# The row of 1/rms: made by two transfers through HBM instead of four transposes and a copy

## The chip, the cores and the metric

The kernel runs on one core of a Trainium2 chip. The metric is the device time of one execution in microseconds, as a median over runs. Smaller is better. The engines are named as in the profile: PE multiplies matrices (TensorE), DVE and ACT do elementwise work (VectorE, ScalarE), POOL is GpSimd, and SP issues transfers.

## The reference

Two layers over 512 tokens of width 1024. Only the first half of a layer concerns the change:

```python
def rmsnorm(x, g):
    xf = x.astype(jnp.float32)
    y = xf * lax.rsqrt(jnp.mean(xf * xf, axis=-1, keepdims=True) + NORM_EPS)
    return (y * g.astype(jnp.float32)).astype(x.dtype)
...
    xn = rmsnorm(x, norm1_g[i])
    proj = xn @ w_in[i]
    u_pool, q, k, v, g_a, g_b = jnp.split(proj, splits, axis=-1)
    ...
    o = diff_attention(q, k, v, lam)
    o = rmsnorm(o, subln_g[i]) * (1.0 - lam_init)
    attn_out = o.transpose(0, 2, 1, 3).reshape(b, s, DIFF_V_WIDTH)
    pool_out = pool_mixer(u_pool, pool_w[i], pool_scale[i])
    merged = jax.nn.sigmoid(g_a) * pool_out + jax.nn.sigmoid(g_b) * attn_out
    x = x + merged @ w_out[i]
```

The pool mixer takes, for each of four groups of channels, the mean over a window of 2, 4, 8 or 16 tokens less the token's own value, and multiplies by a matrix. The attention takes the difference of two softmaxes. Behind it comes a gated feed-forward block with a norm of its own.

## The kernel before

**Products.** Every operand of a product is split in a high and a low part (`split`, L213: a cast on ACT, a subtraction on DVE), and a product is three matmuls: high by high, low by high, high by low (L308 to L310; called a triple here). The names end in h and l: `xh`, `xl` are the tokens, `whi`, `wlo` a piece of weights, `qh`, `ql` the queries and keys, `vh`, `vl` the values, `ah`, `al` the turned attention weights, `uh`, `ul` the windowed means. Weights come in pieces of 512 KB (`raw`, L225), which SP issues in program order, as far ahead as its seven buffers allow.

**The norm.** The weights multiply x itself, and the factor 1/rms of a token is applied to the product. `token_stats` makes it on POOL (L440) as `stats[0][:, 1, :]`, 128 partitions by 4 columns: token on the partition, block of 128 tokens in the column. Queries, keys, values and the attention's gate have tokens on the partitions and use it as a scale. The pool mixer's input and the gate of the pool mixer have tokens along the free dimension, so they need 1/rms as a row of 512 that is the same on all partitions: `rms_rows[layer]`, the second half of the tile `hg`. Its readers are L715 (`up`) and L749 (`ta`) in `merged`. `spread_rms` makes it, once in each layer.

**The attention** goes head by head (3, 2, 1, 0), and in a head by blocks of 128 tokens, t = 0 to 3. Queries and keys of a block are normed, rotated, transposed and scaled (`near`, L546), split to `qh` and `ql`, and `scores(t)` multiplies them; ACT takes the exponentials (L562, `pr`), DVE finishes the softmax, the result is transposed and split to `ah`, `al`, and `weighted(t)` multiplies it with the values (`vh,ah`, then `vl,ah`, then `vh,al`). Its square sum (L606, `mt`), the gate (L610) and a transpose follow, and L629 writes it to `mj`. Except at the start of the program, a transpose is made in two steps: DVE transposes blocks of 32 by 32 (L323), and SP moves the blocks to HBM and back (`turned`: `away<-near` L324, `near<-away` L328, four for each tile). `merged` of a head then makes the windowed means (`up` L715, sums `us` L720, `head` L723, L724, L726) and the two gates (`ta` L749, its tanh L753).

**What sets the order.** A clock counts the columns that PE has been given so far. `later(delay, task)` puts a task on a heap for the time clock + delay, and between triples the due ones are emitted. A scheduler then fixes the order of each engine when the program is built, from the order of emission and the dependencies; on the chip an engine works through its own list and waits at each row for its operands. So a task that is emitted earlier or later can change places with others on each engine.

Of the kernel before, what the change touches and what calls it, by code (L numbers as in the profile page):

```python
# [10 lines left out]
F32 = mybir.dt.float32  # L11
# [7 lines left out]
P = 128  # L19
# [3 lines left out]
NT = S // P  # L23
# [101 lines left out]
def trunk_kernel(  # L125
# [10 lines left out]
    nc = tc.nc  # L136
# [3 lines left out]
    hbm = ctx.enter_context(tc.tile_pool(name="hbm", bufs=1, space=bass.MemoryType.DRAM))  # L140
# [29 lines left out]
    rotary, rms_rows = {}, {}  # L170
# [5 lines left out]
    def head_gains(layer):  # L176

        g = sb.tile([P, 2, S], F32, name="hg", tag="hg")
        rms_rows[layer] = g[:, 1, :]
        cs, sn = rotary[layer] = [g[:, 0, i * VD:(i + 1) * VD].rearrange("p (a t r) -> p a t r", a=2, t=NT) for i in range(2)]  # L180
        row = sb.tile([P, 2, ROT], F32, name="gr", tag="m12")
        for a in range(2):
            nc.sync.dma_start(row[:, a, :], spread(rows[layer][R_QG + QK * a:R_QG + QK * a + ROT]))
        for a in range(2):
            def times(to, table, gains):
                nc.gpsimd.tensor_tensor(to, table, gains.unsqueeze(1).broadcast_to(list(table.shape)), op=ALU.mult)
            times(cs[:, a], cos_t, row[:, a, :])
            for h in range(2):
                here, there = slice(h * HALF, (h + 1) * HALF), slice((1 - h) * HALF, (2 - h) * HALF)
                times(sn[:, a, :, here], sin_t[:, :, here], row[:, a, there])  # L190
        nc.gpsimd.tensor_tensor(gain_column(layer, 0), gain_column(layer, 0), gain_column(layer, 1), op=ALU.mult)
        nc.gpsimd.memset(gain_column(layer, 0)[:ROT], 1.0)
# [68 lines left out]
    def later(delay, what):  # L261
        heapq.heappush(waiting, (clock[0] + delay, count[0], what))
        count[0] += 1
# [50 lines left out]
    def transpose(dst, src):  # L314
        nc.tensor.transpose(dst, src, ident)  # L315
        clock[0] += 2 * P
# [75 lines left out]
    def token(t):  # L392
        return slice(t * P, (t + 1) * P)
# [20 lines left out]
    stats = [None]  # L414
# [87 lines left out]

    def spread_rms(layer):

        row = tr_ps()
        for t in range(NT):
            transpose(row[:, token(t)], stats[0][:, 1, t:t + 1].broadcast_to([P, P]))
        nc.scalar.copy(rms_rows[layer], row)

    for layer in range(L):  # L510
        lam_init = 0.8 - 0.6 * math.exp(-0.3 * layer)
        if layer:
            head_gains(layer)
        later(81600, lambda layer=layer: spread_rms(layer))

        def x_tok(t):
            return [(xh[:, k, token(t)], xl[:, k, token(t)]) for k in range(KD)]
# [588 lines left out]
```

## Time and profile before

| | |
|---|---|
| median of 3 runs | 1378.48 us (1378.47 to 1379.03) |
| the profiled execution | 1377.74 us |
| its span | 1376.0 us, granted TensorE clock 1.000 |
| PE, DVE, ACT, POOL busy | 1370.0, 996.5, 775.1, 130.5 us |
| moved by DMA | 224.07 MB, mean 163 GB/s |

The span is the time from the first to the last event that the profile records; the execution is 1.7 us longer. A row of a timeline gives the start, the duration, the engine, the line in the kernel, the operation, and what it writes and reads; in brackets stands the idle time of its engine ahead of it and what ended it. PE starts a matmul before the one ahead of it has ended, so a matmul of 512 columns has a duration of 0.39 us, and the next one starts 0.23 us behind it. Layer 0 runs to about 700 us, layer 1 from there.

### The profile page before, as it was taken

What the parts mean: (1) busy time and instruction counts of PE and PEld (TensorE: products, weight loads), DVE (VectorE), ACT (ScalarE), POOL (GpSimd) and SP (SyncE); (2) the same over time, 40 slices, a digit from 0 to 9 for tenths busy, and PEclk for the clock granted to TensorE, in tenths of its full rate; (3) what the DMA queues carried; (4) which work ended last, traced back from release to release, by engine and by line L of the source; (5) the groups of instructions that cost most, each with busy time, mean ns of one, the idle gap of its engine ahead of it and who ended that gap; (6) DMA issues with size and microseconds to landing.
All of it is one profiled execution on the core that took longest, in us unless ns stands there. A gap on an engine that the chain in (4) does not pass through costs nothing.

```text
span 1376.0 us, 18657 instructions
## 1 busy us (share of the span) xinstructions
PE 1370.0 (100%) x6238; PEld 1138.1 (83%) x6238; DVE 996.5 (72%) x1787; ACT 775.1 (56%) x1577; POOL 130.5 (9%) x155
## 2 busy tenths in 40 slices
PE   9999999999999999999999999999999999999999
PEld 6888888888888888888888888888888888888887
DVE  7668667676968768678666786765878687686782
ACT  7665564554856545564367755556557665554540
POOL 3010100000101101010010001010001111000100
PEclk9999999999999999999999999999999999999999
DMA  8244454445668968686435455444536788687731
GB/s 312 84 143 121 139 150 143 145 128 151 126 189 193 231 182 222 172 202 189 148 107 163 125 169 166 137 129 137 167 111 139 197 211 221 184 212 175 208 123 62
DMA packets 141072, 224.07 MB, mean 163 GB/s; under 512 B 41392, under 2 KB 88496, under 8 KB 140976
## 3 DMA queue, kind: packets, MB, share of 16 engines
q1 hardware_dynamic: 130320, 186.93, 42.9%
q0 software_dynamic: 9216, 33.56, 14.2%
q10 hardware_dynamic: 1440, 2.39, 0.6%
q8 instruction: 49, 0.80, 0.2%
q14 instruction: 47, 0.39, 0.1%
HBM read 193.59 MB, written 29.23 MB: 162 GB/s over the span
## 4 chain that ended last, share of the span: by engine, by line
PE 98%; DVE 1%; DMA 0%; issue 0%; ACT 0%; SPq 0%; ACTq 0%; DVEq 0%
PE mm L290 17%; PE mm L289 17%; PE mm L291 17%; PE mm L308 15%; PE mm L309 15%; PE mm L310 15%; DMA raw<-in_wts 0%; PE mm L315 0%; DVE xl L476 0%; PE mm L438 0%; DVE wlo L213 0%; PE mm L488 0%; PE mm L486 0%; PE mm L487 0%; DVE sq L427 0%
## 5 line engine op out<-in xcount | busy, mean ns | idle before, releaser
L213 DVE TENSOR_TENSOR wlo<-raw,whi 128x1024 fp32r<-128x1024 f32 (+1 forms) x220 | 267.0, 1218 | 73.9 <-ACT whi L213 73.0
L213 ACT CAST whi<-raw 128x1024 fp32r<-128x1024 f32 (+1 forms) x220 | 229.3, 1052 | 143.8 <-PE mm L291 74.6
L308 PE MATMUL mm<-whi,xh 128*128 128x512 f32 x480 | 188.8, 393 | 0.0
L310 PE MATMUL mm<-whi,xl 128*128 128x512 f32 x480 | 187.2, 390 | 0.0
L309 PE MATMUL mm<-wlo,xh 128*128 128x512 f32 x480 | 187.1, 390 | 0.0
L289 PE MATMUL mm<-whi,xh 128*128 128x512 f32 x384 | 149.6, 390 | 0.0
L291 PE MATMUL mm<-whi,xl 128*128 128x512 f32 x384 | 149.4, 389 | 0.0
L290 PE MATMUL mm<-wlo,xh 128*128 128x512 f32 x384 | 149.4, 389 | 0.0
L290 PE MATMUL mm<-fl,whi 128*128 128x512 f32 (+1 forms) x356 | 137.6, 387 | 0.0
L291 PE MATMUL mm<-fh,wlo 128*128 128x512 f32 (+1 forms) x356 | 137.6, 387 | 0.0
L289 PE MATMUL mm<-fh,whi 128*128 128x512 f32 (+1 forms) x356 | 137.6, 387 | 0.0
L768 DVE TENSOR_TENSOR res<-mm,res 128x512 f32<-128x512 f32 (+1 forms) x145 | 97.8, 679 | 44.0 <-PE mm L291 41.8
L239 POOL DMA_DIRECT2D wlo<-in_wts x64 | 56.1, 876 | 536.6 <-ACT wlo L238 390.3
L353 POOL TENSOR_TENSOR r<-r,mhalf 128x4 f32<-128x4 f32 (+1 forms) x64 | 58.1, 910 | 512.9 <-DVE r L352 493.1
L310 PEld LDWEIGHTS mm<-whi,xl 128*128 128x128 f32 x480 | 90.1, 188 | 19.3
L309 PEld LDWEIGHTS mm<-wlo,xh 128*128 128x128 f32 x480 | 90.3, 188 | 17.3
L308 PEld LDWEIGHTS mm<-whi,xh 128*128 128x128 f32 x480 | 90.2, 188 | 17.3
L308 PE MATMUL mm<-xh,whi 128*128 128x512 f32 x256 | 99.8, 390 | 0.0
L309 PE MATMUL mm<-xl,whi 128*128 128x512 f32 x256 | 99.8, 390 | 0.0
L310 PE MATMUL mm<-xh,wlo 128*128 128x512 f32 x256 | 99.6, 389 | 0.0
L291 PEld LDWEIGHTS mm<-whi,xl 128*128 128x128 f32 x384 | 72.1, 188 | 15.0
L290 PEld LDWEIGHTS mm<-wlo,xh 128*128 128x128 f32 x384 | 72.1, 188 | 15.0
(220 smaller groups left out, 2764.0 us busy)
## 6 DMA issues: line engine op xcount, KB each, us to landing
raw<-in_wts SPq DMA_DIRECT2D x243, 512.0 KB, 4.1
wlo<-in_wts POOLq DMA_DIRECT2D x64, 512.0 KB, 6.4
away<-near SPq DMA_DIRECT2D x73, 256.0 KB, 2.3
near<-away SPq DMA_DIRECT2D x292, 64.0 KB, 2.8
away<-near SPq DMA_DIRECT2D x29, 128.0 KB, 2.0
near<-away SPq DMA_DIRECT2D x116, 32.0 KB, 2.2
pwr<-in_pool_w ACTq DMA_DIRECT2D x8, 256.0 KB, 2.8
out<-res SPq DMA_DIRECT2D x7, 256.0 KB, 2.0
```

Of the source, the lines that this page charges most:

```text
L213: return nc.scalar.copy(hi, src), nc.vector.tensor_sub(lo, src, hi.bitcast(F32))
L239: nc.gpsimd.dma_start(lo.rearrange("p a b -> p (a b)"), wts[piece_no], accum_op=ALU.add)
L289: nc.tensor.matmul(acc, lhsT=ah, rhs=bh, start=start, stop=False, **check)
L290: nc.tensor.matmul(acc, lhsT=ah, rhs=bl, start=False, stop=False, **check)
L291: last = nc.tensor.matmul(acc, lhsT=al, rhs=bh, start=False, stop=stop, **check)
L308: nc.tensor.matmul(acc, lhsT=ah, rhs=bh, start=i == 0, stop=False)
L309: nc.tensor.matmul(acc, lhsT=ah, rhs=bl, start=False, stop=False)
L310: last = nc.tensor.matmul(acc, lhsT=al, rhs=bh, start=False, stop=i == n - 1)
L353: nc.gpsimd.tensor_tensor(r, r, mhalf[:, :width], op=ALU.pow)
L768: return nc.vector.tensor_add(res[d][:, cs], acc, res[d][:, cs])
```

## The change

`spread_rms` no longer transposes on PE and copies on ACT. SP writes the 512 values to a row in HBM (128 partitions by 4 columns of 4 bytes, turned by the access pattern), and a second transfer on SP, which waits for the first to land, reads the row back onto all partitions. The task is put on the heap 64800 columns ahead in place of 81600, and the transposes' 1024 columns no longer advance the clock.

```diff
     def spread_rms(layer):
 
-        row = tr_ps()
-        for t in range(NT):
-            transpose(row[:, token(t)], stats[0][:, 1, t:t + 1].broadcast_to([P, P]))
-        nc.scalar.copy(rms_rows[layer], row)
+        row = hbm.tile([NT, P], F32, name="row", tag="row", bufs=2)
+        nc.sync.dma_start(row.rearrange("t p -> p t"), stats[0][:, 1, :])
+        nc.sync.dma_start(rms_rows[layer], row.rearrange("t p -> (t p)").partition_broadcast(P))
 
     for layer in range(L):
         lam_init = 0.8 - 0.6 * math.exp(-0.3 * layer)
         if layer:
             head_gains(layer)
-        later(81600, lambda layer=layer: spread_rms(layer))
+        later(64800, lambda layer=layer: spread_rms(layer))
```

The lines below are one shorter, so L606 of before is L605 of the changed kernel. The order of the engines changes with it. On SP, in layer 1, where the queries and keys of the first head are sent away, it was:

```order
L225 DMA raw<-in_wts 128x1024 x2
L328 DMA near<-away 32x4x128 x4
L225 DMA raw<-in_wts 128x1024 x9
L324 DMA away<-near 128x512 x2
L328 DMA near<-away 32x4x128 x8
```

and it is now:

```order
L225 DMA raw<-in_wts 128x1024 x2
L328 DMA near<-away 32x4x128 x4
L225 DMA raw<-in_wts 128x1024 x9
L506 DMA row<-stats 128x4x1
L507 DMA hg<-row 128x512
L324 DMA away<-near 128x512 x2
L328 DMA near<-away 32x4x128 x8
```

The two transfers stand ahead of the first two away-transfers. In layer 0 they stand among the weight pieces: four pieces and two other loads, the write, two pieces, the read, eleven pieces.

On ACT, in layer 1, second head, around the cast of `ah` for `weighted(2)` (128x384), with the tanh of the first gate `ta` and the casts of both halves of `uh`, it was:

```order
L606 ACTIVATE mt,sso<-mm 128x256
L213 CAST uh<-us 128x512
L213 CAST ah<-pr 128x384
L213 CAST uh<-us 128x512
L606 ACTIVATE mt,sso<-mm 128x256
L753 ACTIVATE ta<-ta 128x512
L213 CAST whi<-raw 128x1024 x3
L213 CAST ah<-pr 128x512
```

and it is now:

```order
L605 ACTIVATE mt,sso<-mm 128x256
L568 ACTIVATE rc<-st 128x1
L213 CAST uh<-us 128x512
L752 ACTIVATE ta<-ta 128x512
L213 CAST ah<-pr 128x384
L213 CAST uh<-us 128x512
L605 ACTIVATE mt,sso<-mm 128x256
L213 CAST whi<-raw 128x1024
L213 CAST ah<-pr 128x512
```

The tanh has moved from behind this cast to ahead of it. On PE the same place was, from the end of the product that the gate `ta` reads to the first matmuls of `weighted(2)`:

```order
L308 MATMUL mm<-xh,whi 128x512
L309 MATMUL mm<-xl,whi 128x512
L310 MATMUL mm<-xh,wlo 128x512
L308 MATMUL mm<-vh,ah 128x256
L309 MATMUL mm<-vl,ah 128x256
L308 MATMUL mm<-xh,whi 128x512
L309 MATMUL mm<-xl,whi 128x512
L310 MATMUL mm<-xh,wlo 128x512
L310 MATMUL mm<-vh,al 128x256
```

and it is now:

```order
L308 MATMUL mm<-xh,whi 128x512
L309 MATMUL mm<-xl,whi 128x512
L310 MATMUL mm<-xh,wlo 128x512
L308 MATMUL mm<-vh,ah 128x256
L309 MATMUL mm<-vl,ah 128x256
L310 MATMUL mm<-vh,al 128x256
```

The triple that stood between the matmuls of `ah` and that of `al` has gone behind them. On DVE, in the same place, the subtraction `al` stood ahead of the multiply `ta` (L749); now `ta` (L748) comes first, then the last window sum, `head` and the two rows that finish `us`, and then `al`.

On ACT, in the same head around the cast of `qh` for `scores(1)`, it was:

```order
L692 ACTIVATE vh<-mm,stats 128x256
L695 ACTIVATE tb<-mm,stats 128x256
L546 ACTIVATE near<-near,scale 128x2x4x32
L696 ACTIVATE tb<-tb 128x256
L213 CAST qh<-near 128x4x128
L562 ACTIVATE pr,st<-mm,mx 128x128 x2
```

and it is now:

```order
L691 ACTIVATE vh<-mm,stats 128x256
L628 ACTIVATE mj<-near,scale 128x128 x2
L694 ACTIVATE tb<-mm,stats 128x256
L695 ACTIVATE tb<-tb 128x256
L561 ACTIVATE pr,st<-mm,mx 128x128 x2
L545 ACTIVATE near<-near,scale 128x2x4x32
L568 ACTIVATE rc<-st 128x1
L213 CAST qh<-near 128x4x128
```

The exponentials of `scores(0)` have moved ahead of the scale and the cast.

## The prediction

> **What bounds the kernel now.** First the engines' busy times on the page, then the chain that ended last, then the list of PE's waits.
>
> ```profile
> span 1376.0 us, 18657 instructions
> PE 1370.0 (100%) x6238; PEld 1138.1 (83%) x6238; DVE 996.5 (72%) x1787; ACT 775.1 (56%) x1577; POOL 130.5 (9%) x155
> PE 98%; DVE 1%; DMA 0%; issue 0%; ACT 0%; SPq 0%; ACTq 0%; DVEq 0%
> PE mm L406 <- DVE us L719: 1.2, 1, 1.2
> PE mm L495 <- DVE xh L475: 0.9, 1, 0.9
> PE mm L438 <- DVE sq L434: 0.4, 1, 0.4
> ```
>
> PE is busy for 1370.0 of 1376.0 us and is 98% of the chain. The three waits that the list names add up to 2.5 us. So only two things can change the time: columns that PE no longer multiplies, and new moments in which PE finds its operand unfinished. The rest of the prediction is a search for those moments. The profiled execution took 1377.74 us, 1.7 us more than its span and 0.74 us less than the median 1378.48; I work out a difference against the profiled one and put it on the median.
>
> **What goes from PE and ACT.** The four transposes of layer 0 in PE's timeline, those of both layers in the chain, and the copy in ACT's timeline:
>
> ```profile
> 54.62 0.60 PE L315 MATMUL mm<-ident,stats 128*128 128x128 f32 x4
> 54.78 0.44 PE mm L315 x4
> 729.29 0.44 PE mm L315 x4
> 56.16 0.60 ACT L508 COPY hg<-mm 128x512 f32<-128x512 f32 x1
> ```
>
> The chain counts 0.44 us for each group of four. PE had no wait there, so both groups come off the end: 2 × 0.44 = **−0.88 us**. The copy (0.60 us in the row shown, one in each layer) is on ACT, which is busy 56% of the span; it stood in no wait of PE, so it is worth nothing itself.
>
> **What the two transfers cost.** The writes wait for the POOL instruction that makes 1/rms, and everything behind them on SP waits too (rows of the engines' timelines, of the DMA issues and queues):
>
> ```profile
> 24.18 1.95 POOL L440 TENSOR_TENSOR stats<-stats,mhalf 128x4 f32<-128x4 f32 x1 [1.23 <-DVE stats L439]
> 703.55 1.04 POOL L440 TENSOR_TENSOR stats<-stats,mhalf 128x4 f32<-128x4 f32 x1 [54.48 <-DVE stats L439]
> 709.09 1.84 SPq L324 DMA_DIRECT2D away<-near  x2
> 717.07 0.52 ACT L546 ACTIVATE near<-near,scale 128x256 f32<-128x256 f32 x1
> 727.76 0.22 PE L308 MATMUL mm<-qh 128*128 128x128 f32 x1
> away<-near SPq DMA_DIRECT2D x1, 64.0 KB, 1.5
> gr<-in_rows SPq DMA_DIRECT2D x4, 16.0 KB, 5.6
> q1 hardware_dynamic: 130320, 186.93, 42.9%
> 797.98 0.68 DVE L715 TENSOR_TENSOR up<-mm,hg 128x512 f32<-128x512 f32 x1
> ```
>
> In layer 1 the pair stands on SP between a piece of weights and the away-transfers of the first head (709.09). The row can leave at 704.6, when POOL is done, so 4.5 us pass before anything behind it is due. Behind it stand those away-transfers and their way back; ACT scales what came back at 717.07 and PE multiplies it at 727.76. After the scale only a cast and a subtraction follow, so I put some 6.8 us more of slack there: the row's landing may take about 11 us before PE notices. No transfer of 4-byte elements is in this trace. From below, the nearest row is the 64 KB transfer that landed in 1.5 us, from above the slowest small one, 16 KB in 5.6 us. A worse end comes from the queue's row: 130320 packets took 42.9% of 16 × 1376 us, 72 ns each; 512 elements as 512 packets are 2.3 us over sixteen engines, but 37 us if one engine had them all. I take 4 us: hidden, **0 us** (at 37 us it would be about 26 us; that is a rival below). In layer 0 POOL ends at 26.1 and SP holds the weight pieces behind it for some 3 to 5 us after; the buffered pieces are first cast many us later, and I take 0. The reader of the row in layer 1 runs at 797.98, over 90 us behind, so its arrival costs nothing.
>
> The Trainium skill speaks against this edit: its page "DMA: Bandwidth & Descriptors", section "Rules for kernel authors", says that a strided last dimension is lowered to one descriptor for each element. This trace has no such transfer; by that rule alone the 512 elements are the 512 packets counted above, and the sum is the same as long as they are spread. The same page's "Anatomy of one DMA — SWDGE (gpsimd) path" gives about 2.0 us of fixed time for any transfer, mostly the receipt of the write; the 1.5 us row here is below that, and it was measured on another path.
>
> **What moves.** With 1024 columns fewer on the planner's clock, and the row asked for sooner, later tasks are emitted at other points, and the static order of every engine changes. I compared at each place how much PE work lies between an operand's last step and the matmul that reads it. Cover shrinks to nothing at one place, and gets thin at two others.
>
> **The second head of layer 1, token block 2 (about 808 us).** The rows of before, from the timelines of the engines, the last two from the chain:
>
> ```profile
> 804.74 0.51 ACT L213 CAST ah<-pr 128x384 fp32r<-128x384 f32 x1
> 808.19 0.67 DVE L720 TENSOR_TENSOR us<-us 128x512 f32<-128x512 f32 x1
> 808.64 0.39 PE L310 MATMUL mm<-xh,wlo 128*128 128x512 f32 x1
> 808.86 0.28 PE L308 MATMUL mm<-vh,ah 128*128 128x256 f32 x1
> 809.10 0.40 PE L308 MATMUL mm<-xh,whi 128*128 128x512 f32 x1
> 808.78 0.55 DVE L213 TENSOR_TENSOR al<-pr,ah 128x384 fp32r<-128x384 f32 x1
> 809.34 0.67 DVE L724 SCALAR_TENSOR_TENSOR us<-us,up 128x496 f32<-128x496 f32 x1
> 809.92 0.17 DVE L726 TENSOR_TENSOR us<-head,up 128x16 f32<-128x16 f32 x1
> 810.01 0.68 DVE L749 TENSOR_TENSOR ta<-mm,hg 128x512 f32<-128x512 f32 x1
> 811.20 0.62 ACT L753 ACTIVATE ta<-ta 128x512 f32<-128x512 f32 x1
> 815.18 0.39 PE L310 MATMUL mm<-xh,wlo 128*128 128x512 f32 x1
> 814.98 0.62 ACT ah L213
> 815.65 0.39 PE mm L308
> ```
>
> Before, ah was cast at 804.74, four us ahead of PE's first use at 808.86. In the new order ACT has the tanh of the gate, ta, between the cast of uh and the cast of ah. That tanh waits for the multiply ta on DVE, and the multiply for the product that PE ends immediately before it wants ah (809.03 = 808.64 + 0.39). On DVE the subtraction al now stands behind ta, the last window sum, head and the two that finish us. And PE, which used to have a triple of matmuls between ah and al, now has vh,ah, vl,ah, vh,al in a row. Step by step: ta starts at 809.07 and takes 0.68; the tanh starts at about 809.8 and takes 0.62, the cast 0.51 more: it ends at 810.9, 2.0 us after PE wanted it. On DVE an instruction starts some 0.08 before the one ahead has ended (us of 0.67 at 808.19, the next at 808.78), so from start to start: ta 0.60, us 0.59, head 0.09 (as the small us at 809.92), us 0.58, us 0.09. So al starts at 811.02 and ends at 811.57. PE runs vh,al at 811.6, where it would have been at 809.10: **+2.5 us**. Since ta waits for PE's own product, no idle engine can run ahead to hide this: it is a loop PE–DVE–ACT–PE. Its bounds are 1.9 (hardly more than the cast's lateness counts) and 2.9 (the small memsets between cost something as well).
>
> One short wait goes: the chain shows the cast of ah at 814.98 and PE at 815.65 only, 0.24 us after 815.41, where its previous matmul (815.18, and the 0.23 us to a next start that PE's rows show throughout) would have let it start. In the new order one more triple is ahead of it and fewer casts before that cast: **−0.24 us**. What is late next there is nothing: some 5 us of matmuls lie ahead.
>
> **Scores of blocks 1 and 2 of the same head (777 and 785 us).**
>
> ```profile
> 769.49 0.44 DVE L323 STREAM_TRANSPOSE near<-mt 128x256 f32<-128x256 f32 x1
> 769.96 0.38 ACT L606 ACTIVATE mt<-mm 128x256 f32<-128x256 f32 x1 [1.27 <-DVE near L323]
> 776.25 0.69 DVE L213 TENSOR_TENSOR ql<-near,qh 128x512 fp32r<-128x512 f32 x1 [0.91 <-ACT qh L213]
> 777.26 0.28 PE L308 MATMUL mm<-qh 128*128 128x256 f32 x1
> 777.37 0.28 PE L309 MATMUL mm<-ql,qh 128*128 128x256 f32 x1
> 783.64 0.47 ACT L692 ACTIVATE vh<-mm,stats 128x256 fp32r<-128x256 f32 x1 [0.46 <-PE mm L310]
> 784.12 0.33 PE L308 MATMUL mm<-qh 128*128 128x384 f32 x1
> ```
>
> At block 1, ql ended at 776.94 and PE wanted it at 777.37: 0.43 us of slack. Now scores(0) comes one triple (0.68 us) later on PE, the two exponentials of it stand ahead of the scale and cast of block 1 on ACT, and the softmax's small steps ahead of ql on DVE. If everything else ran as before, qh would end at 777.65 and ql at 778.35: 1.0 us late. Against it: the eviction mt that waited on ACT for the transpose of 769.49 until 769.96 no longer has that transpose ahead, and the chain behind it (r, qn, vh) can be about a microsecond sooner; then the wait is nothing. I take **+0.2 us**, with 0 and 1.0 as ends. At block 2, the scale and cast now stand behind vh, which ran at 783.64 when its product was done; cast and subtraction end at about 785.2 and 785.9, and PE, which now has five more matmuls of 0.227 us ahead, comes at 785.25 and 785.8: **+0.1 us**, ends 0 and 0.4.
>
> Sum: −0.88 − 0.24 + 2.5 + 0.2 + 0.1 = **+1.68 us**. 1377.74 + 1.68 = 1379.42 beside the profiled execution; on the median 1380.2 us.
>
> **The rivals.**
> - *All is hidden, and only PE's saving remains*: the new order would have to be harmless at 808 us, for example because PE comes there later relative to ACT and DVE. −0.88 − 0.24 = −1.12, or 1377.4 us. For it speaks that PE waits so rarely; against it that the tanh depends on PE's own product, whenever PE comes.
> - *The second inversion bites (slower)*: at block 1 scores the wait is the full 1.0 us, at block 2 0.4, and the loop at 808 us is at its 2.9: 2.9 + 1.4 − 1.12 = +3.2, or 1381.7 us. It becomes decisive when qh at 777 us ends over 0.4 us after PE comes and the loop is at its upper end. For it: the slack was 0.43 us. Against it: the earlier eviction.
> - *The row is slow on SP (slower)*: 512 pieces of 4 bytes land later than 11 us in layer 1, and each us beyond is one on PE; at 37 us +26, some 1406 us. It decides from about 14 us of landing on. Against it: no transfer in this trace that small took more than 5.6 us.
> - *Faster by over 0.2%*: 2.76 us would have to go; the transposes are 0.88, and every wait of PE together 2.5 at the very start, which the change doesn't touch. Hardly possible.
>
> **How the numbers follow.** 0.2% of 1378.48 is 2.76 us, about what a measurement of this kernel can tell from no change: 1375.72 to 1381.24. Forecast (1379 to 1381.2) 0.64; all hidden 0.14; second inversion 0.14; slow row 0.06; faster 0.02. So faster 0.02, same 0.78, slower 0.20. The predicted time is the forecast's, 1380.2. The range takes in the first rival (1377.4, and 0.2 under it) and the second (1381.7): 1377.2 to 1381.8, leaving out the slow row and a part of the tails.
>
> **What the new profile would show.** PE without the eight transposes. In layer 1's second head a wait of PE of 2 to 3 us, in two parts, at the first vh,ah of block 2 and at vh,al behind it, with the tanh directly ahead of the cast of ah on ACT; no wait there would prove the first rival right. A wait at ql of about 777 us between 0 and 1 us. On SP the row's write leaving just after POOL, its readback 2 to 6 us behind, and the away-transfers of the first head not much later than 709 us; a landing of over 11 us would make the prediction wrong.

## The result, and the profile after

The changed kernel took 1389.94 us (median of 5 runs, 1388.6 to 1391.31), against 1379.03 us for the kernel before (5 runs, 1378.47 to 1379.21): 10.9 us more, a ratio of 1.0083 with a 95% interval of 1.0072 to 1.0094. The profiled execution took 1389.56 us. The prediction was 1380.2 us, with a range of 1377.2 to 1381.8: the sign was right, the size far too small.

From the page of the changed kernel, the span, the engines' busy times and the chain:

```profile
span 1387.8 us, 18652 instructions
PE 1373.4 (99%) x6230; PEld 1138.2 (82%) x6230; DVE 995.4 (72%) x1787; ACT 772.9 (56%) x1575; POOL 128.1 (9%) x155
PE 87%; DVE 5%; DMA 3%; ACT 2%; issue 1%; POOL 1%; SPq 1%; ACTq 0%; DVEq 0%; POOLq 0%
```

PE has eight instructions fewer, and yet is no longer 98% of the chain but 87%. PE's waits by line, engine and operand (us in total, times, longest) say where:

```profile
PE mm L308 <- ACT qh L213: 2.4, 1, 2.4
PE mm L308 <- ACT ah L213: 2.1, 1, 2.1
PE mm L315 <- ACT lam L203: 1.4, 1, 1.4
...
PE mm L308 <- ACT pr L561: 1.1, 2, 0.8
PE mm L310 <- DVE al L213: 0.7, 1, 0.7
...
PE mm L309 <- DVE ql L213: 0.3, 1, 0.3
PE mm L310 <- DVE a L213: 0.2, 1, 0.2
```

The three waits left out (L406, L495 and L438) were there before, L495 with 0.2 us less. New are `ah` and `al` (2.8 us together, the loop of the prediction, at about 816 us on this clock), `qh` and `ql` (2.7 us, at 784 us, where 0.2 was predicted), and `lam` and `pr` (2.5 us, at 46 to 60 us in layer 0, where nothing was predicted). The list counts from a matmul's modelled end; counted from start to start, a wait costs some 0.2 us more.

SP's timeline has the reason for the last two groups; the POOL row that makes 1/rms in layer 1 stands with it, and last, for comparison, SP's row of the kernel before with the way back:

```profile
26.36 0.38 SPq L506 DMA_DIRECT2D row<-stats  x1
26.78 0.98 SPq L225 DMA_DIRECT2D raw<-in_wts  x2
36.15 0.33 SPq L507 DMA_DIRECT2D hg<-row  x1
...
708.18 0.38 SPq L506 DMA_DIRECT2D row<-stats  x1
716.57 0.33 SPq L507 DMA_DIRECT2D hg<-row  x1
716.99 0.86 SPq L324 DMA_DIRECT2D away<-near  x2
722.33 4.29 SPq L328 DMA_DIRECT2D near<-away  x8
```

```profile
707.12 1.04 POOL L440 TENSOR_TENSOR stats<-stats,mhalf 128x4 f32<-128x4 f32 x1 [54.49 <-DVE stats L439]
```

```profile
711.11 4.67 SPq L328 DMA_DIRECT2D near<-away  x8
```

The read can only leave when the write has landed: 9.8 us behind it in layer 0 and 8.4 us in layer 1, where the prediction had taken 4. What stands behind the read on SP waits with it. In layer 1 the away-transfers leave at 717.0, 7.9 us later than before, and their way back begins 11.2 us later (722.33 against 711.11); only some 3.6 us of that is the delay that layer 0 had already made (POOL is done at 708.16 and not at 704.59). In layer 0 the eleven weight pieces behind the read leave from 36.5 us on. Even the two pieces that stand between write and read suffer: they land 12.8 and 13.7 us after their issue, where the median of such a piece was 4.0 us before, and from 28.5 to 36.1 us the DMA engines are busy for 0.83 of the time and move only 33 GB/s. ACT's timeline shows the cast of the first:

```profile
39.67 1.05 ACT L213 CAST whi<-raw 128x1024 fp32r<-128x1024 f32 x1 [7.31 <-DMA raw<-in_wts]
```

and the timeline of the kernel before shows both at the same place:

```profile
31.93 2.11 ACT L213 CAST whi<-raw 128x1024 fp32r<-128x1024 f32 x2
```

ACT stood 7.3 us idle for weights that it had cast at 31.93 before. They were not "many us" ahead of their use, as the prediction had it.

### The profile page after: what moved, and what is told of

Its sections match the earlier page's. It is cut to its first block, busy times and chain, and to the rows that moved or that the text cites. A ratio compares the mean times of both kernels' runs of the same rounds, so it can differ in the third digit from the quotient of the medians.

```text
span 1387.8 us, 18652 instructions
## 1 busy us (share of the span) xinstructions
PE 1373.4 (99%) x6230; PEld 1138.2 (82%) x6230; DVE 995.4 (72%) x1787; ACT 772.9 (56%) x1575; POOL 128.1 (9%) x155
## 4 chain that ended last, share of the span: by engine, by line
PE 87%; DVE 5%; DMA 3%; ACT 2%; issue 1%; POOL 1%; SPq 1%; ACTq 0%; DVEq 0%; POOLq 0%
PE mm L290 17%; PE mm L289 17%; PE mm L291 17%; PE mm L309 12%; PE mm L310 12%; PE mm L308 12%; DMA raw<-in_wts 1%; DVE wlo L213 1%; POOL r L353 1%; ACT qn L644 1%; DMA away<-near 1%; ACT whi L213 1%; DVE near L323 0%; DMA near<-away 0%; DVE mx L560 0%
```

## The experiments

Two theories at first. **Q**: what is lost is lost on SP's queue, behind the two transfers. **O**: it is lost by the new order of PE, ACT and DVE. They can be told apart, because the order of PE, ACT and DVE is the same, row for row, in the traces of the changed kernel and of the kernel without the transfers. Whether the new delay or the 1024 columns that are gone from the clock move the order is not shown: every run below that puts the columns back has the old delay too.

Each kernel is compared with runs of the kernel before on the same chip; medians of one group can be compared directly, those of two groups by their distance to the kernel before.

### First group: is it the queue or the order? (before: 1377.93 us)

**no_row.** In `spread_rms`:

```diff
-        row = hbm.tile([NT, P], F32, name="row", tag="row", bufs=2)
-        nc.sync.dma_start(row.rearrange("t p -> p t"), stats[0][:, 1, :])
-        nc.sync.dma_start(rms_rows[layer], row.rearrange("t p -> (t p)").partition_broadcast(P))
+        nc.gpsimd.memset(rms_rows[layer], 1.0)
```

> The changed kernel without its two transfers: POOL sets the row to 1.0 instead, so the pool mixer and its gate are computed with a wrong factor. The order of PE, ACT and DVE is that of the changed kernel, row for row. Theory Q (SP's queue: the weight pieces and away-transfers behind the two transfers come late): the waits of PE at 46 to 60 us and at 762 to 785 us vanish, only the loop at about 816 us stays, 2.5 us or 3.8 us with the slow matmuls behind it, and the eight transposes stay saved: 1380 to 1382 us. Theory O (the new order of ACT, DVE and PE makes all of the waits): 1387 to 1390 us.

Measured: 1382.73 us (1380.82 to 1384.7), ratio 1.0035 [1.0022, 1.0047]. The waits at 46 to 60 us are gone; of those in layer 1 these are left:

```profile
PE mm L308 <- ACT ah L213: 2.1, 1, 2.1
PE mm L310 <- DVE al L213: 0.5, 1, 0.5
PE mm L309 <- DVE ql L213: 0.3, 1, 0.3
```

Q holds for over half of the loss: the changed kernel is 10.9 us over the kernel before, this one 4.8. It took 0.7 us more than the range expected for Q; the granted clock, in the last section, has a part in that.

**row_l0** and **row_l1.** The transfers in one layer alone:

```diff
+        if layer != 0:            # row_l1: != 1
+            nc.gpsimd.memset(rms_rows[layer], 1.0)
+            return
         row = hbm.tile([NT, P], F32, name="row", tag="row", bufs=2)
```

> The changed kernel with the two transfers in layer 0 alone; in layer 1 POOL sets the row to 1.0. Same order of PE, ACT and DVE. Theory Q: the waits at 46 to 60 us come back and cost 3.5 to 4 us over the kernel without any transfer, those at 762 to 785 us stay away: 1384 to 1386 us. Theory O: as without transfers, 1387 to 1390 us.

> The changed kernel with the two transfers in layer 1 alone; in layer 0 POOL sets the row to 1.0. Same order of PE, ACT and DVE. Theory Q: no wait at 46 to 60 us, the waits at 762 to 785 us are there, some 4 us over the kernel without any transfer: 1384 to 1386 us. Theory O: 1387 to 1390 us, or 3.7 us less if layer 0's waits alone are SP's.

Measured: 1385.82 us (ratio 1.0055 [1.0042, 1.0067]) with the transfers in layer 0, 1388.40 us (1.0076 [1.0063, 1.0089]) in layer 1. Layer 0 costs 3.1 us over no_row, with the waits for `lam` (1.5) and `pr` (1.1) back; layer 1 costs 5.7 us, with `qh` (3.2 in two waits) back. Both layers have their own price, as Q says; in row_l1 it was above the expected range. They do not add up: 3.1 and 5.7 make 8.8, but the changed kernel loses only some 6 us to the queue. The traces fit that: in row_l1 the write took 10.8 us to land and the away-transfers left 6.2 us later than in no_row (715.94 against 709.71); in the changed kernel they left 4.8 us later than in row_l0 (716.99 against 712.19), where layer 0 is late as well.

**old_order.** The transfers as in the change, and the columns back on the clock:

```diff
+        clock[0] += 4 * 2 * P
...
-        later(64800, lambda layer=layer: spread_rms(layer))
+        later(81600, lambda layer=layer: spread_rms(layer))
```

> The changed kernel, with the clock advanced by the 1024 columns of the transposes and the old delay of 81600: the transfers stay where they are on SP, and the tanh is behind the cast of ah of block 2 again. Theory Q: the wait at about 816 us goes (2.5 us, or 3.8 with the slow matmuls), SP's share stays: 1385 to 1387.5 us. Theory O: 1377.5 to 1380 us.

Measured: 1388.84 us (ratio 1.0076 [1.0062, 1.0089]), no better than the change. This missed both expectations. The wait at 808 us is gone, but this order has waits for `ah` and `al` at other places, 80 and 765 us, when the queue is late. Nor is it the order of the kernel before: beyond the transposes, rows of PE, ACT and DVE have changed places, so it is a third order. With the queue late, this order gains nothing; the two losses overlap.

### Second group: what makes the landing late, and what is the loop? (before: 1377.98 us)

**no_row_old_order** is old_order without the transfers.

> The order with the transposes' columns still on the clock, without the transfers (POOL sets the row to 1.0). Theory Q: the 10 us that this order with transfers lost are all SP's, so 1377 to 1378.5 us. Rival (this order has waits of its own at 75, 758 and 777 us): 1380 us or more.

Measured: 1378.57 us (ratio 1.0006 [0.9997, 1.0015]). Against old_order that is 10.3 us less: in this order nearly all of the loss is the queue's. Against no_row it is 4.2 us less: that is the price of the changed kernel's order when nothing is late on SP, against this third order and with what the granted clock adds. The expected range ended at 1378.5; the transposes' 0.88 us are not gained. These new waits stand against them:

```profile
PE mm L308 <- ACT qh L213: 0.7, 1, 0.7
PE mm L309 <- DVE ql L213: 0.3, 1, 0.3
```

**row_contig.** The write keeps the order of SBUF, 16 bytes from each partition, and nothing else changes; the readers get the values in that order and not in the tokens':

```diff
-        nc.sync.dma_start(row.rearrange("t p -> p t"), stats[0][:, 1, :])
+        nc.sync.dma_start(row.rearrange("t p -> (t p)").rearrange("(p t) -> p t", t=NT), stats[0][:, 1, :])
```

> The changed kernel, but the write keeps the order of SBUF, 16 bytes from each partition, so 128 pieces and not 512; the row is read in the wrong order. Order of the engines as in the changed kernel. Theory D (the 4-byte pieces make the write slow): the write lands in 2 to 3 us in both layers, and the time falls by 2 to 4 us, to 1385 to 1388 us. Rival (it waits for what is ahead of it in its queues, or for HBM): it lands in 8 to 10 us still, 1388.5 to 1391 us.

Measured: 1384.00 us (1381.14 to 1384.4), ratio 1.0042 [1.0028, 1.0055]. SP still waits for POOL, but the read now leaves 1.4 us behind the write:

```profile
26.86 0.33 SPq L506 DMA_DIRECT2D row<-stats  x1
...
28.27 0.35 SPq L507 DMA_DIRECT2D hg<-row  x1
...
704.74 0.33 SPq L506 DMA_DIRECT2D row<-stats  x1
706.15 0.33 SPq L507 DMA_DIRECT2D hg<-row  x1
709.21 1.83 SPq L324 DMA_DIRECT2D away<-near  x2
```

The away-transfers are back at 709.2 us, and the waits of layer 0 and for `qh` are gone. The time fell by 4.9 us, more than the 2 to 4 that were expected, and what is left over no_row, 1.2 us, is within the spread of the two kernels' runs. So the wait for POOL on SP, 10 us long in layer 0, and the pair of transfers cost nothing that these runs can tell: the price of the queue is the slow landing of 512 pieces of 4 bytes. That the write waits for what stands ahead of it is ruled out, because here it stands at the same place.

**no_row_gate_behind.** no_row, and the gate's multiply and tanh tied behind the subtraction and cast of block 2 (`cast_of` keeps what `split` returns for a head and block; the gate is that of head 3, computed during the second head; a third tie, not printed, keeps the second cast of `uh` behind that of `ah`):

```diff
+                first = cast_of.get((1, 2, 2)) if (layer, j, c) == (1, 3, 0) else None
+                with tc.issue_after(first[1].ins) if first else ExitStack():
-                nc.vector.tensor_mul(ta, acc, rms_rows[layer])
+                    nc.vector.tensor_mul(ta, acc, rms_rows[layer])
...
+                    behind = cast_of[1, 2, 2][0] if (layer, j, c) == (1, 3, 0) else None
+                    with tc.issue_after(behind.ins) if behind else ExitStack():
-                    nc.scalar.activation(ta, ta, AF.Tanh, scale=0.5)
+                        nc.scalar.activation(ta, ta, AF.Tanh, scale=0.5)
```

> The kernel without transfers (row set to 1.0), with one more edit: on DVE the multiply of the first gate, and on ACT its tanh, are put behind the subtraction al and the cast ah of block 2 of the second head of layer 1. Nothing else moves on PE, ACT or DVE but a small memset. Theory A (the loop of PE, DVE and ACT at 808 us is what is left): 3.5 us of waits go, and the slow matmuls behind them where the clock falls: 1377.5 to 1379.5 us, against 1382.7 without this edit. Rival (the cast and subtraction are late for another reason, such as the turned pr): 1382 to 1383 us.

Measured: 1381.18 us (1379.84 to 1384.25, 11 runs), ratio 1.0026 [1.0017, 1.0034]: 1.6 us less than no_row, between the two expectations, and not clear of the spread of no_row's five runs. The wait for `ah` is gone, and that for `al` has grown to take its place: counted from start to start, PE loses 2.8 us here where it lost 3.1 in no_row. The rest of the difference fits the granted clock, which stood at half for 6.8 us behind the wait in no_row's profile and not at all in this one (last section). In order: PE's wait, and the rows of ACT and DVE.

```profile
PE mm L311 <- DVE al L213: 2.7, 1, 2.7
```

```profile
808.09 0.51 ACT L213 CAST ah<-pr 128x384 fp32r<-128x384 f32 x1 [0.97 <-DMA pr<-away]
```

```profile
806.50 0.68 DVE L713 TENSOR_TENSOR up<-mm,hg 128x512 f32<-128x512 f32 x1
...
812.28 0.56 DVE L213 TENSOR_TENSOR al<-pr,ah 128x384 fp32r<-128x384 f32 x1
```

`ah` is ready at 808.6, but DVE comes to `al` only at 812.28: it works through the window sums first, without a gap. Before, `up` stood at 804.10. The lateness begins with the scores of block 3, which PE now makes later: between them and the product of block 2, `weighted(2)`, stand 50 matmuls of weights, where 56 stood before. DVE's reduction of them before:

```profile
795.00 0.69 DVE L561 TENSOR_REDUCE mx<-mm 128x1 f32<-128x512 f32 x1
```

and in this kernel:

```profile
797.33 0.69 DVE L559 TENSOR_REDUCE mx<-mm 128x1 f32<-128x512 f32 x1
```

So there were two chains of almost the same length, and the prediction's loop was only one of them. (The other by itself, with the gate left ahead, was not tried.)

**late_transfers.** The whole computation; the write and the read tied on SP behind later away-transfers, the columns on the clock, and the gate behind:

```diff
+        clock[0] += 4 * 2 * P
+        later(60000, away)
+        later(90000, back)
```

where `away` and `back` issue the write and the read behind the last `near<-away` issued so far.

> The whole computation: the two transfers are tied on SP behind away-transfers that come later, the write some 26 us after the place of the transposes, the read 13 us behind it, the transposes' columns stay on the clock, and the gate's multiply and tanh stand behind al and ah. If queue and loop are all that the change lost: 1377 to 1378.5 us, the saving of the transposes with nothing given back. If the transfers cost wherever they are: over 1380 us.

Measured: 1383.88 us (ratio 1.0041 [1.0028, 1.0054]), a miss. The tasks put on the heap at other times moved the order again, and PE waits for `ah` (1.6 us) at 135 us and for `qh` and `al` in layer 1. It doesn't tell what late transfers cost, only that an edit of the emission isn't a neutral one here. Its writes left at 80 and 770 us, and they too took 10.8 us to land (the median of the two).

### Third group: the two mechanisms by themselves (before: 1378.51 us)

**al_first.** no_row_gate_behind, and the last two window sums behind `al` on DVE:

```diff
+                first = cast_of.get((1, 2, 2)) if (layer, j, c) == (1, 3, 1) and step in (4, 8) else None
+                with tc.issue_after(first[1].ins) if first else ExitStack():
-                nc.vector.tensor_add(cur[:, 16:], prev[:, 16:], prev[:, 16 - step:16 + S - step])
+                    nc.vector.tensor_add(cur[:, 16:], prev[:, 16:], prev[:, 16 - step:16 + S - step])
```

> The kernel without transfers (row set to 1.0) and with the gate's multiply and tanh behind al and ah, with one more edit: on DVE the last two window sums of the pool mixer's second half are put behind the subtraction al as well. Order of PE unchanged. Theory V (DVE, busy without a gap from 797 to 812 us, reaches al late whatever the gate does): al ends at about 810.3 us, the wait of 2.7 us falls to 0.3 or less, 1378 to 1379.5 us. Rival (al waits for an operand): the wait stays, 1380.5 to 1382 us.

Measured: 1378.59 us (1377.52 to 1380.13, 11 runs), ratio 1.0001 [0.9992, 1.0010]: 3.1 us less than no_row_gate_behind, each taken from the kernel before of its group. DVE's row:

```profile
808.97 0.55 DVE L213 TENSOR_TENSOR al<-pr,ah 128x384 fp32r<-128x384 f32 x1
```

and neither `ah` nor `al` is in the list of PE's waits. That settles the place at 808 us: moving one multiply and one tanh on their own leaves nearly the whole wait, and with two sums of DVE moved too the wait is gone and the kernel is level with the one before, 4.7 us under no_row.

**row_spread.** The changed kernel with the values 64 bytes apart in HBM:

```diff
+        nc.gpsimd.memset(rms_rows[layer], 1.0)
-        row = hbm.tile([NT, P], F32, name="row", tag="row", bufs=2)
+        row = hbm.tile([NT, P, 16], F32, name="row", tag="row", bufs=2)
-        nc.sync.dma_start(row.rearrange("t p -> p t"), stats[0][:, 1, :])
-        nc.sync.dma_start(rms_rows[layer], row.rearrange("t p -> (t p)").partition_broadcast(P))
+        nc.sync.dma_start(row[:, :, 0].rearrange("t p -> p t"), stats[0][:, 1, :])
+        nc.sync.dma_start(rms_rows[layer][:NT, :P], row[:, :, 0])
```

> The changed kernel with a row in HBM in which each of the 512 values has 64 bytes of its own; POOL sets the row in SBUF to 1.0, and the second transfer reads the 512 values back to four partitions only, and waits as before. Same order of PE, ACT and DVE. If each small write costs by itself, the write lands in 8 to 10 us as in the changed kernel. If the sixteen values that share 64 bytes hinder each other, it lands in 2 to 3 us.

Measured: 1382.62 us (1380.18 to 1384.28, 8 runs), ratio 1.0031 [1.0021, 1.0041], 4.1 us over the kernel before, within the spread of no_row's 4.8. The DMA issues (KB, and median us to landing) of the changed kernel, of row_contig and of row_spread, in this order:

```profile
row<-stats SPq DMA_DIRECT2D x2, 2.0 KB, 9.1
```

```profile
row<-stats SPq DMA_DIRECT2D x2, 2.0 KB, 1.4
```

```profile
row<-stats SPq DMA_DIRECT2D x2, 2.0 KB, 2.0
```

512 pieces of 4 bytes land in 2.0 us if each has 64 bytes of its own. So their number and size do not make the landing slow by themselves, and neither does lying side by side, as the 128 pieces of 16 bytes in row_contig do: it takes 4-byte pieces that lie side by side. In the changed kernel neighbours in HBM come from different partitions; whether pieces of 4 bytes are as slow when neighbours come from one partition was not tried.

**contig_old_clock** and **contig_gate_behind.** The whole computation. Both write the row in the order of SBUF and let the readers L715 and L749 take it through a permuted view:

```diff
-            nc.vector.tensor_mul(up[:, 16:], acc, rms_rows[layer])
+            nc.vector.tensor_mul(in_blocks(up[:, 16:]), in_blocks(acc), rms_rows[layer].rearrange("p (q t) -> p t q", t=NT))
```

The first adds the columns to the clock, the second has the edits of al_first.

> The whole computation: the write keeps the order of SBUF (16 bytes from each partition), the two readers on DVE read the row through a permuted view, and the transposes' columns stay on the clock. If the slow landing and the moved order are all that the change lost: as the same order without transfers, 1378 to 1379.5 us, 10 us below the changed kernel. If the strided view makes the readers dear, or the read back costs on SP: over 1381 us.

> The whole computation, with the write in the order of SBUF and the permuted view, the changed kernel's order of PE, and the edits of al_first on ACT and DVE. What is left is the wait of about 0.9 us for qh and ql at 777 us, and the saving of the transposes: 1378 to 1379.5 us. If something else of the new order costs, 1380 us and more.

Measured: 1380.05 us (ratio 1.0014 [1.0005, 1.0023]), 0.6 us over its range, and 1379.35 us (1.0008 [0.9999, 1.0016]), within it; before, 1378.51 us. The 10.9 us of the change are down to 1.5 and 0.8 us, but neither beats the kernel before: four transposes on PE remain as cheap as any of the transfers. The permuted view is not free: the 32 multiplies that read the row take 1.06 us each on DVE, where they took 0.69 before. Both profiles add two waits for `ml`, the low part of the operand behind the gates, of 0.23 us each at 341 and 1024 us; that the longer multiplies make them was not tested. A wait for `al` of 0.4 and 0.8 us at 811 us is left, too.

## Why the prediction was wrong

**The bound and the transposes** were read rightly: PE had no slack, and each new wait costs in full. The saving of 0.88 us is there, but the smaller waits that came with the order eat it; no kernel without the transposes is measurably faster than the one before.

**The row's landing** is the step that failed. The prediction took "4 us: hidden, 0 us" from the bounds 1.5 and 5.6 us of other small transfers, and kept a slow row as a rival with a chance of 0.06. It took 9.8 and 8.4 us, and its price is 5 to 6 of the 10.9 us (the changed kernel is 10.9 us over the kernel before, no_row 4.8 and row_contig 6.0). The upper bound was a misreading: the 5.6 us in the row of `gr` are the median of four transfers, and the slowest of these four took 10.1 us in the same trace. The count was right, 512 pieces as 512 packets: under 512 bytes the changed kernel has 768 packets more than row_contig, 384 in a layer, which is 512 less 128. But the price of a packet was not: the engines were done with all of them in about two us, and the rest is waiting for the landing. No row of the trace resembled 4-byte pieces, and the range should have reached the rival's side.

**What a late row does** was wrong as well. The rival put the point of decision at 11 us, from the slack of the first scores of layer 1; by that, a landing of 8.4 us would have been hidden as well. Those scores did wait for nothing; but ACT and DVE take their rows in order and carried the lateness through a chain of over 60 us. Some rows of the chain of the changed kernel:

```profile
716.99 5.28 DMA away<-near
...
726.19 2.09 DMA near<-away
...
735.86 3.88 DMA near<-away
...
777.15 1.02 POOL r L353
...
783.33 0.52 ACT qh L213
```

PE's wait comes at 783.9, for the `qh` of the second head. And layer 0, costed at "0" because the buffered pieces were "first cast many us later", lost 3.1 us: two of the pieces were cast from 31.93 on, 5.8 us after POOL was done (26.13), and now came at 39.67.

**The loop at 808 us** was mis-sized by a little, and half understood. Predicted were 2.5 us, with 1.9 and 2.9 as ends. In the changed kernel PE goes from 816.09 to 818.62 and from 818.84 to 819.85, where 0.23 and 0.12 are its pace:

```profile
816.09 0.39 PE L310 MATMUL mm<-xh,wlo 128*128 128x512 f32 x1
818.62 0.39 PE L308 MATMUL mm<-vh,ah 128*128 128x256 f32 x1 [2.14 <-ACT ah L213]
818.84 0.28 PE L309 MATMUL mm<-vl,ah 128*128 128x256 f32 x1
819.85 0.38 PE L310 MATMUL mm<-vh,al 128*128 128x256 f32 x1 [0.73 <-DVE al L213]
```

That is 2.30 + 0.89 = 3.2 us, over the upper end. DVE was still at a window sum when the gate's product ended, so `ta` starts 0.3 us behind it (816.81 against 816.48), and from the start of `ta` to that of `al` it takes 2.42 us and not 1.95, with the memsets that the sum left out. The tanh ahead of the cast did what was said, but no_row_gate_behind shows that DVE would have been nearly as late without it. The order listing showed `al` behind the window sums, and the prediction counted only the rows from `ta` on; it did not follow DVE back to the scores of block 3.

**Scores of blocks 1 and 2**: in no_row, 0.7 us at block 1, counted from start to start (0.2 predicted, ends 0 and 1.0), and nothing at block 2 (0.1). **The short wait** at 815 us did go. So the order alone, without the queue and at full clock, comes to −0.88 − 0.24 + 3.2 + 0.7 = +2.8 us, where +1.68 was predicted; row_spread's three runs at clock 1.000 were 1.7 to 2.8 us over the kernel before. This part of the prediction was near, and its mechanism held but for the second chain.

**The clock behind a wait** is a term that the sum does not have. Behind the wait of the loop PE's clock was halved for 3.4 us in the changed kernel's profile, some 1.6 us more, and for 6.8 us in no_row's; the last section has the rows.

## What to carry to other kernels

A transfer that turns small data element by element must be judged by its landing, and by what stands behind it on the issuing queue; here 2 KB held a queue for 8 to 11 us. The slack of the first consumer is not the slack of a delay: engines that work in order carry it on until the bound engine meets it, here over 60 us later. When a wait is explained by one moved instruction, look whether the next chain behind it is as long, before its removal is counted as a gain. And the column of a view has to be known before it serves as a bound: a median of four is no maximum.

## What the runs showed of the hardware

**Writes that share a neighbourhood in HBM.** The windows of the changed kernel in layer 1, the write, the wait, and the read (us; busy time of PE, PEld, DVE, ACT and POOL, with their instructions; then PE's granted clock, the DMA share and GB/s):

```profile
708.18:709.40 1.22, 1.22 (x7) 1.00 (x6) 0.70 (x5) 0.00 (x0) 0.63 (x1) 1.00 0.19 2
709.40:710.30 0.90, 0.90 (x6) 0.74 (x5) 0.00 (x0) 0.49 (x2) 0.90 (x2) 1.00 0.02 0
710.30:716.50 6.20, 6.20 (x29) 5.15 (x28) 4.48 (x13) 4.78 (x20) 1.46 (x2) 1.00 0.00 0
716.50:722.30 5.80, 5.80 (x28) 4.79 (x27) 5.21 (x10) 4.18 (x12) 0.12 (x1) 1.00 0.42 131
```

The DMA engines are done with the 512 pieces after about two us, and then nothing moves for over six us until the landing is reported. The Trainium skill, page "DMA: Bandwidth & Descriptors", section "Specifications", says that transfers under 512 bytes make the engine read, modify and write; its "Anatomy of one DMA — SWDGE (gpsimd) path" says that most of a transfer's fixed time is the receipt of the write, and gives some 2 us. The trace agrees that the time lies behind the last piece, but the whole transfer takes 8.4 to 10.8 us where 4-byte pieces are neighbours (row_l1 and late_transfers have the longest), 1.4 us in pieces of 16 bytes and 2.0 us at a distance of 64 bytes. That the receipt makes it so long is not shown, and whether the sharing of 64 bytes or of a wider stretch decides was not tried.

**The granted clock after a wait.** Right behind the waits at 816 to 820 us, PE ran at half its clock:

```profile
815.00:820.70 5.70, 2.83 (x15) 2.05 (x14) 5.31 (x17) 1.65 (x3) 0.00 (x0) 0.98 0.29 82
820.70:824.20 3.50, 3.50 (x12) 2.79 (x11) 0.70 (x2) 1.32 (x3) 0.54 (x1) 0.54 0.24 54
```

3.5 us at a granted clock of 0.54 cost about 1.6 us more. The Trainium skill, page "TensorE: Matmul & The Clock Gate", section "What's actually happening", describes a clock that is halved after an idle window of about 3.4 us, by a window that runs freely. Here waits of 2.1 and 0.7 us with two matmuls between them, shorter than that window, were enough, and the measurement decides. The slow stretch does not come in every profile: row_l1 shows the slow stretch behind its wait at 782 us (0.50 from 783.9 to 787.3) and none behind 816. no_row and row_contig have the same order and the same waits at 812 us; the profile of the first shows a stretch at half the clock behind them, that of the second none:

```profile
812.36:819.19 6.83, 6.33 (x19) 5.17 (x20) 2.90 (x10) 2.66 (x5) 0.54 (x1) 0.50 0.24 58
```

```profile
813.00:816.40 3.40, 3.40 (x18) 2.99 (x19) 1.33 (x5) 1.58 (x4) 0.54 (x1) 1.00 0.32 71
```

6.83 us at 0.50 cost 3.4 us, and the profiled execution of no_row took 3.3 us longer (1384.47 against 1381.14 us), though it has no transfers at all. The clocks of the single runs say the same: of the eight runs of row_spread, the three with a mean clock of 1.000 took 1380.2 to 1381.3 us, the five with 0.997 to 0.999 took 1382.3 to 1384.3. So 1 to 3 us (an estimate, from the medians and the runs at clock 1.000) of the 4.8 and 6.0 that no_row and row_contig lost are the clock, not the waits themselves. al_first, which has no such wait, had 1.000 in all its 11 runs. Not every kernel's runs sort so clearly: row_l0's five, at 0.998 to 1.000, lie within 0.9 us, and three of the 33 runs of the kernel before in the third group show 0.998 or 0.999 at 1378.9 to 1379.1 us. A window that runs freely would fit a stretch that comes and goes from run to run; it was not tested by itself.
